# A row-maximum kernel: the first load as two transfers, partitions 0 to 15 and then 16 to 127

## The chip, the core and the metric

The kernel runs on one core of a Trainium2 chip. The metric is the time of one execution on the device, in microseconds (us). Runs of the kernel before agree to less than 0.1 us.

## The reference

The input is a float32 array of 32 x 512 x 1024, and the output is its maximum along the last axis:

```python
def reference(x):
    return np.max(x, axis=-1).astype(np.float32)
```

Flattened, there are 16,384 rows of 1024 numbers, 67.1 MB, and one number comes out of each row.

## The kernel before, in words

The rows are spread over 128 partitions, 128 rows for each partition. `BLOCKS` (lines 13 to 16) cuts these 128 into a first block of 112 and a second of 16. Within a block each partition owns consecutive rows of the input, so a load of n rows per partition reads n x 4096 consecutive bytes for each partition. In the first block the loads have 14, 13, 12, 11, 9, 8, 8, 7, 6, 5, 5, 4, 4, 3 and 3 rows per partition, in the second 2, 2, 2 and then nine times 1; the last row of each partition is loaded in two halves.

All loads but the very last half go into `ring` (line 39), a buffer with place for 45 rows per partition. Each load takes the next n places; where they would run over the end, it begins at place 0 again. So the loads of 14, 13 and 12 rows (39 places) fit side by side, and the load of 11 begins at the start again, where the 14 rows lay.

The loop at lines 53 to 60 goes over the loads. Line 57 issues a load from the queue of the sync engine (SP); line 58 takes its maximum on the vector engine (DVE) with one instruction into `res`. SP issues loads in the order of the program. A load whose places were used before waits for the reduction that read them; this is why the load of 11 rows waits for the first reduction. The framework gives the transfers eight completion semaphores in turn, so a transfer also waits for the one eight before it. DVE reduces the loads in the same order, each as soon as its load has landed.

At the end, lines 64 to 70 load and reduce the last row in two halves, and the ACT queue stores `res` in two pieces, 56 KB (line 73) and 8 KB (line 75).

The lines in question are:

```python
            xc = ring[:, at:at + n, :]
            nc.sync.dma_start(out=xc, in_=xb[:, b:b + n, :])
            reduce = nc.vector.reduce_max(out=res[:, first + b:first + b + n], in_=xc, axis=X)
```

Of the kernel before, what the change touches and what calls it, by code (L numbers as in the profile page):

```python
# [1 line left out]

# [4 lines left out]


F32 = mybir.dt.float32

BLOCKS = [
    [14, 13, 12, 11, 9, 8, 8, 7, 6, 5, 5, 4, 4, 3, 3],
    [2, 2, 2, 1, 1, 1, 1, 1, 1, 1, 1, 1],
]
RING = 45
SYNC = mybir.DependencyInfo(mybir.DependencyClass.Sync, mybir.DependencyReason.DATA)


@with_exitstack
def kernel(
    ctx: ExitStack,
    tc: tile.TileContext,
    x: bass.AP,
    out: bass.AP,
):
    nc = tc.nc
    P = 128
    X = mybir.AxisListType.X  # L30

    xf = x.flatten_outer_dims()
    N, D = xf.shape
    H = D // 2
    I = N // P
    of = out.flatten_outer_dims()

    once = ctx.enter_context(tc.tile_pool(name="once", bufs=1))
    ring = once.tile([P, RING, D], F32)
    res = once.tile([P, I], F32)  # L40

    PAD = 16
    tail = once.tile([P, PAD + H], F32)

    at = first = 0
    views = []
    for loads in BLOCKS:
        S = sum(loads) + (loads is BLOCKS[-1])
        xb = xf[first * P:(first + S) * P, :].rearrange("(p i) d -> p i d", p=P)
        dst = bass.AP(tensor=of.tensor, offset=of.offset + first * P, ap=[[S, P], [1, S]])  # L50
        views.append((dst, res[:, first:first + S]))
        b = 0
        for n in loads:
            if at + n > RING:
                at = 0
            xc = ring[:, at:at + n, :]
            nc.sync.dma_start(out=xc, in_=xb[:, b:b + n, :])  # L57
            reduce = nc.vector.reduce_max(out=res[:, first + b:first + b + n], in_=xc, axis=X)  # L58
            at += n
            b += n  # L60
        first += S
    assert first == I

    if at + 1 > RING:
        at = 0
    half = ring[:, at, :H]
    nc.sync.dma_start(out=half, in_=xb[:, b, :H])
    nc.sync.dma_start(out=tail[:, PAD:], in_=xb[:, b, H:])
    nc.vector.reduce_max(out=tail[:, PAD - 1:PAD], in_=half, axis=X)  # L69
    nc.vector.reduce_max(out=res[:, I - 1:], in_=tail[:, PAD - 1:], axis=X)  # L70


    store = nc.scalar.dma_start(out=views[0][0], in_=views[0][1])
    tc.add_manual_dep(store.ins, reduce.ins.name, SYNC, reason="behind the loads")
    nc.scalar.dma_start(out=views[1][0], in_=views[1][1])


# [1 line left out]
_INS = ['x']  # L79
_OUTS = [((32, 512), 'float32')]  # L80


# [23 lines left out]
```

## Time and profile before

| What | Value |
|---|---|
| Median of 3 runs | 164.99 us (164.98 to 165.05) |
| The profiled execution | 165.17 us |
| Span of its profile, first to last instruction | 163.4 us |
| DVE busy | 139.0 us, 85% of the span |
| Bytes read | 67.11 MB, 411 GB/s over the span |
| First load | 7168 KB, 19.6 us from issue to landing |
| First reduction starts | at 20.31 us, takes 15.09 us |

Times in the profile count from the start of the span. "Busy" is the time in which an engine executed. The sync engine is shown as SPq where it issues transfers; those instructions are not counted as busy. The arrow in a line such as `res<-ring` reads from right to left, output from input. A transfer is cut into packets, and here a packet of the first load is the whole of one partition's part, 57,344 bytes. In the windows a packet is counted with all its bytes where it starts, so short windows go above what the hardware can move and then show zero; only a stretch of several microseconds has a true rate.

### The profile page before, as it was taken

Reading aid. Unit: us, or ns where it says so; the run is one execution under the profiler, and the core shown is the slowest. Engines: PE = TensorE matmul, PEld = TensorE weight load, DVE = VectorE, ACT = ScalarE, POOL = GpSimd, SP = SyncE. Lnnn points to the kernel's source line nnn. Section 1 sums busy time; section 2 is a strip of 40 time slices with the busy share of each in tenths; the row PEclk is TensorE's granted clock in tenths of the full one; section 3 lists DMA queues with packets and bytes.
Section 4 is the critical chain, followed back from the end, with each engine's and each line's share of the span. In section 5 each row is a group of like instructions: output and inputs, shape, how many; then the busy total and the mean of one; then the engine's idle time right before and its main releaser. Section 6 shows DMA issues by size and latency. Waiting matters only on the chain.

```text
span 163.4 us, 117 instructions
## 1 busy us (share of the span) xinstructions
DVE 139.0 (85%) x29; POOL 0.2 (0%) x4
## 2 busy tenths in 40 slices
DVE  0000099989998999999999999999999999999994
POOL 0000000000000000000000000000000000000000
DMA  6999999999989989999989999999999999999990
GB/s 225 449 449 449 433 417 417 417 401 529 433 385 430 452 386 432 433 433 441 457 385 481 401 442 422 409 438 421 446 409 425 437 410 422 427 407 409 409 355 16
DMA packets 4464, 67.18 MB, mean 411 GB/s; under 512 B 752, under 2 KB 752, under 8 KB 2160
## 3 DMA queue, kind: packets, MB, share of 16 engines
q1 hardware_dynamic: 4176, 67.11, 96.6%
q10 hardware_dynamic: 288, 0.07, 0.2%
HBM read 67.11 MB, written 0.07 MB: 411 GB/s over the span
## 4 chain that ended last, share of the span: by engine, by line
DVE 49%; DMA 48%; SPq 1%; issue 0%
DMA ring<-in_x_dram 48%; DVE res L58 48%; SPq L57 1%; DVE res L70 0%; DVE tail L69 0%
## 5 line engine op out<-in xcount | busy, mean ns | idle before, releaser
L58 DVE TENSOR_REDUCE res<-ring 128x1 f32<-128x1024 f32 (+12 forms) x27 | 137.7, 5165 | 22.1 <-DMA ring<-in_x_dram 22.1
L70 DVE TENSOR_REDUCE res<-tail 128x1 f32<-128x513 f32 x1 | 0.7, 686 | 0.0
L69 DVE TENSOR_REDUCE tail<-ring 128x1 f32<-128x512 f32 x1 | 0.7, 682 | 0.0
L90 POOL MEMSET const-bfloat16-1.0<- 128x1 bf16 x1 | 0.1, 102 | 0.0
L90 POOL MEMSET const-uint8-127<- 128x1 uint8 x1 | 0.1, 102 | 0.0
L90 POOL MEMSET const-float32-0.0<- 128x1 f32 x1 | 0.1, 99 | 0.2 <-issue 0.2
L90 POOL MEMSET const-float32-1.0<- 128x1 f32 x1 | 0.1, 99 | 0.0
## 6 DMA issues: line engine op xcount, KB each, us to landing
ring<-in_x_dram SPq DMA_DIRECT2D x2, 4096.0 KB, 25.6
ring<-in_x_dram SPq DMA_DIRECT2D x1, 7168.0 KB, 19.6
ring<-in_x_dram SPq DMA_DIRECT2D x1, 6656.0 KB, 34.9
ring<-in_x_dram SPq DMA_DIRECT2D x1, 6144.0 KB, 48.9
ring<-in_x_dram SPq DMA_DIRECT2D x1, 5632.0 KB, 28.5
ring<-in_x_dram SPq DMA_DIRECT2D x2, 2560.0 KB, 38.4
ring<-in_x_dram SPq DMA_DIRECT2D x1, 4608.0 KB, 24.7
ring<-in_x_dram SPq DMA_DIRECT2D x9, 512.0 KB, 13.8
```

Of the source, the lines that this page charges most:

```text
L57: nc.sync.dma_start(out=xc, in_=xb[:, b:b + n, :])
L58: reduce = nc.vector.reduce_max(out=res[:, first + b:first + b + n], in_=xc, axis=X)
L69: nc.vector.reduce_max(out=tail[:, PAD - 1:PAD], in_=half, axis=X)
L70: nc.vector.reduce_max(out=res[:, I - 1:], in_=tail[:, PAD - 1:], axis=X)
L90: nc = _bacc.Bacc("TRN2", target_bir_lowering=False, num_devices=1)
```

## The change

For the first load alone (the load of 14 rows), line 57 becomes two transfers from the same queue: first partitions 0 to 15, then partitions 16 to 127. With 16 partitions each of the sixteen DMA engines may get one descriptor. The reduction of the first load now waits for both. All other loads stay as they are, and so do all reductions. The program has one transfer more on the sync engine's queue, and the completion semaphores that the later transfers use move on by one.

```diff
             xc = ring[:, at:at + n, :]
-            nc.sync.dma_start(out=xc, in_=xb[:, b:b + n, :])
+
+            for p, q in ((0, 16), (16, P)) if first + b == 0 else ((0, P),):
+                nc.sync.dma_start(out=xc[p:q], in_=xb[p:q, b:b + n, :])
             reduce = nc.vector.reduce_max(out=res[:, first + b:first + b + n], in_=xc, axis=X)
```

## The prediction

> **What bounds the kernel now.** I read the chain of waits first, then the waits, then the timeline, and last the windows over the first microseconds.
>
> ```profile
> DVE 49%; DMA 48%; SPq 1%; issue 0%
> ...
> DVE res L58 <- DMA ring<-in_x_dram: 22.1, 5, 20.3
> ...
> 20.31 15.09 DVE L58 TENSOR_REDUCE res<-ring 128x14 f32<-128x14336 f32 x1 [20.31 <-DMA ring<-in_x_dram]
> 36.05 14.02 DVE L58 TENSOR_REDUCE res<-ring 128x13 f32<-128x13312 f32 x1 [0.65 <-DMA ring<-in_x_dram]
> 50.58 12.95 DVE L58 TENSOR_REDUCE res<-ring 128x12 f32<-128x12288 f32 x1 [0.51 <-DMA ring<-in_x_dram]
> 63.91 30.14 DVE L58 TENSOR_REDUCE res<-ring 128x11 f32<-128x11264 f32 x3 [0.38 <-DMA ring<-in_x_dram]
> 94.27 65.48 DVE L58 TENSOR_REDUCE res<-ring 128x8 f32<-128x8192 f32 x21 [0.21 <-DMA ring<-in_x_dram]
> ...
> ring<-in_x_dram SPq DMA_DIRECT2D x1, 7168.0 KB, 19.6
> ```
>
> The first line is the chain's split: half VectorE (DVE), half transfers. The second says that of DVE's 22.1 us of waiting on loads, 20.3 is one wait, for the first load. The timeline shows what follows: from 20.31 on DVE reduces almost without a break (gaps of 0.65, 0.51, 0.38 and 0.21, together 1.75 us) until 160. So the end is the landing of the first load plus about 141 us of DVE work and four small gaps. One microsecond on the first landing is one microsecond on the end, unless the 1.75 us of gaps absorb some of it. The last line is that load's 19.6 us from issue (at 0.73) to landing.
>
> How are these 19.6 us made up? The windows have columns window, length, DVE busy, POOL busy, clock, DMA share, GB/s; a packet is put at its start.
>
> ```profile
> 1.25:1.50 0.25, 0.00 (x0) 0.00 (x0) 1.00 0.00 0
> 1.50:1.75 0.25, 0.00 (x0) 0.00 (x0) 1.00 2.98 918
> 1.75:2.00 0.25, 0.00 (x0) 0.00 (x0) 1.00 4.59 1376
> 2.00:2.25 0.25, 0.00 (x0) 0.00 (x0) 1.00 1.39 459
> 2.25:2.50 0.25, 0.00 (x0) 0.00 (x0) 1.00 1.19 459
> 2.50:2.75 0.25, 0.00 (x0) 0.00 (x0) 1.00 1.07 459
> 2.75:3.00 0.25, 0.00 (x0) 0.00 (x0) 1.00 0.00 0
> ...
> 4.00:8.00 4.00, 0.00 (x0) 0.00 (x0) 1.00 1.06 459
> ```
>
> A row of the first load is one partition's 14 x 1024 x 4 = 57,344 bytes. One such packet in a quarter microsecond reads 229 GB/s, so the five filled windows hold 4, 6, 2, 2 and 2 packets: all sixteen DMA engines start their first row between 1.5 and 2.75 us. After that the stream is full: 459 GB/s at a share of 1.06 is 433 GB/s at share 1, or 27.1 per engine, so **a row takes 57,344 / 27.1 = 2.12 us**. 128 rows on 16 engines are 8 rows each, 16.9 us. Issue 0.73, first packets about 1 us later, 16.9 us of rows, and some 1.3 us of stagger and slow first rows give the landing near 20; DVE starts at 20.31.
>
> [...]
>
> **The change part by part.**
>
> *First piece, 16 rows[...].* [...] I take 8.46.
>
> *Second piece, 112 rows, seven to each engine.* [...] How the rows are dealt out isn't in the trace. I take contiguous sevens: engine e writes partitions 16+7e to 22+7e. [...] I take the middle of 10.6 and 14.8, 12.7, and take off 0.7, about half of the 1.3 us of stagger and slow first rows[...]: **+12.0**.
>
> *One more issue on SP.* An issue takes 0.37 to 0.43 us with 0.05 between (chain: 0.73, 1.15, 1.63). The second piece goes out at about 1.15, the loads of 13 and 12 at about 1.6 and 2.1. The sixteen engines have rows until 17 us at least; that covers it, cost 0. Without this cover 0.42. The load of 11 still waits for the first reduce; it now waits on two transfers as well, landed by then.
>
> *One more wait on DVE.* The first reduce waits for two transfers. If that takes an instruction of its own it is like SP's wait instructions at L57, 17 ns: 0.02. Everything else on DVE is queued behind it and stays in order and size.
>
> *What the delay does later.* Fast engines hold three loads and can't run dry: the load of 11 goes out after the first reduce, near 47 us, before any engine is through its 39 rows per partition (20.4 MB, 47 us at 433 GB/s, after the 6 us lost on its first row). The late engines set the second landing too, so I expect the gap of 0.65 to stay and no delay to be given back; at most 1.75 us would be. DVE's 139 us stay. Late next is every reduce, by the same amount.
>
> Sum: 163.4 + 12.0 = 175.4 of span. The profiled execution took 165.17, so 177.2; the median of the runs is 164.99, 0.18 below it, so 177.0.
>
> **Rivals.** *[...]better dealt:* if the second piece's rows meet no more than they must, the cost is 8.5 - 0.7 = +7.8, 172.8. [...] *The change doesn't do what it says:* the first piece is given to four engines, four rows each, and those then have 11 rows: 23.3 us, +6.4, 171.4. [...] *Other side, faster:* [...] sixteen single rows are handed out faster than 128. Then the stagger between 1.5 and 2.75 us shrinks; it holds at most 1.3 us, and I price it at 0.6: 164.4. It decides if the first piece's rows take about 2.1 us; from 2.7 us a row on (2.12 + 0.6) the gain is gone. For: the first issue takes 371 ns against 327 of others[...]. *No change:* [...] the starts stay staggered, 165.0. *Dealt sixteen at a time:* 8 x 8.46 = 67.7 us, +50.8, 215.8.
>
> **How the numbers follow.** A measurement of this kernel can tell about 0.2% (0.3 us) from no change. Contiguous sevens 0.50 (174.5 to 183.5); better dealt 0.20 (171.5 to 174.5); four engines 0.10 (169.5 to 171.5); sixteen at a time 0.06; faster 0.08; no change 0.06. Slower is 0.50 + 0.20 + 0.10 + 0.06 = 0.86. The likeliest gives 177.0. The range 169.5 to 183.5 holds the first three, 0.80.
>
> **What would show it.** In the changed profile: the first piece lands 9 to 11 us after its issue (wrong if 3 to 4); few bytes start in the windows from 3 to 9 us; the second piece lands near 32; the first reduce starts near 32.3; the four later gaps are as now; the last reduce ends 12 us later. A first reduce within half a microsecond of 20.31 makes the whole argument wrong. A first piece of 9 to 11 us with a first reduce at 28 means better dealing; near 70, sixteen at a time. A late first reduce with a smaller shift of the end would mean that the gaps gave some back.

## The result, and the profile after

The changed kernel takes 183.71 us (median of 6 runs, 183.31 to 184.32) against 165.02 before (6 runs, 164.87 to 165.15): a ratio of 1.114, 95% interval 1.112 to 1.116, **18.7 us slower**. I forecast 177.0 and a range up to 183.5, so the direction was right and the size was not: 12.0 us were forecast, 18.7 came, and the time lies 0.2 us above the range.

The views of the changed kernel that answer to those of before are, in this order, the split of the chain, DVE's wait for loads, the timeline of the first reductions and the issues of the second and the first piece:

```profile
DVE 60%; DMA 37%; another core or an unknown queue 1%; SPq 0%; issue 0%; DVEq 0%
...
DVE res L60 <- DMA ring<-in_x_dram: 40.6, 5, 39.0
...
38.98 15.09 DVE L60 TENSOR_REDUCE res<-ring 128x14 f32<-128x14336 f32 x1 [38.98 <-DMA ring<-in_x_dram]
54.63 14.02 DVE L60 TENSOR_REDUCE res<-ring 128x13 f32<-128x13312 f32 x1 [0.57 <-DMA ring<-in_x_dram]
69.16 12.95 DVE L60 TENSOR_REDUCE res<-ring 128x12 f32<-128x12288 f32 x1 [0.51 <-DMA ring<-in_x_dram]
82.49 30.14 DVE L60 TENSOR_REDUCE res<-ring 128x11 f32<-128x11264 f32 x3 [0.38 <-DMA ring<-in_x_dram]
112.84 65.46 DVE L60 TENSOR_REDUCE res<-ring 128x8 f32<-128x8192 f32 x21 [0.21 <-DMA ring<-in_x_dram]
...
ring<-in_x_dram SPq DMA_DIRECT2D x1, 6272.0 KB, 37.7
...
ring<-in_x_dram SPq DMA_DIRECT2D x1, 896.0 KB, 10.6
```

The "unknown queue" in the first line is the gaps of about half a microsecond ahead of the second and the third reduction, for which the timeline names the loads. All of the loss lies ahead of the first reduction. It starts at 38.98 instead of 20.31, 18.67 later; every duration and every later gap is as before, but for the gap of 0.65, which is 0.57. So 0.1 us is given back, and the span is 18.5 longer. The first piece lands 10.6 us after its issue, where I expected 9 to 11. The second lands 37.7 us after its issue, at 38.9, where I expected 32. The excess is in the second piece.

The windows say more. "Row" is meant here as in the forecast, one partition's part of the load. A step is sixteen rows that start together, as many as there are DMA engines. A window that holds all sixteen starts of one step has 16 x 57,344 bytes in it, so GB/s times length is about 918. Then the DMA share times the length is the **mean duration of a row** in that step. For the kernel before, the first two steps:

```profile
1.40:2.90 1.50, 0.00 (x0) 0.00 (x0) 1.00 1.87 612
4.40:5.30 0.90, 0.00 (x0) 0.00 (x0) 1.00 2.35 1019
```

These are 1.87 x 1.50 = 2.81 us and 2.35 x 0.90 = 2.12 us; the first row is slower than those that follow. The eight steps of the changed kernel, the 16-row piece first, then the seven of the 112-row piece:

```profile
1.40:2.90 1.50, 0.00 (x0) 0.00 (x0) 1.00 4.96 612
...
8.50:10.30 1.80, 0.00 (x0) 0.00 (x0) 1.00 2.59 510
13.50:14.50 1.00, 0.00 (x0) 0.00 (x0) 1.00 4.12 918
17.60:18.60 1.00, 0.00 (x0) 0.00 (x0) 1.00 2.98 918
20.60:22.80 2.20, 0.00 (x0) 0.00 (x0) 1.00 1.51 417
23.90:26.00 2.10, 0.00 (x0) 0.00 (x0) 1.00 1.87 437
27.50:30.00 2.50, 0.00 (x0) 0.00 (x0) 1.00 1.62 367
31.50:34.00 2.50, 0.00 (x0) 0.00 (x0) 1.00 1.57 367
```

The row means are 7.4, then 4.7, 4.1, 3.0, 3.3, 3.9, 4.1 and 3.9 us. A row of the second piece takes 3.9 us, 1.8 times the normal 2.12, **on the mean of all engines**. The rows within a step differ too. By the packets of the trace, in the step at 13.50 all sixteen took 4.09 to 4.25 us. In the one at 17.60 two took 4.19 and fourteen 2.60 to 2.99, in the one at 20.60 two took 3.79 and 3.87 and the others 3.23 to 3.38. These are the two short steps: only they have two late rows and a faster rest.

So the theory to test: (a) the second piece is dealt out in contiguous sevens; (b) the cost comes from which partitions are written in the same step; (c) some sets of sixteen partitions slow all their rows, others only two of them. The rivals: another dealing, with worse sets; a cost in reading memory; a cost of having more transfers; and for (c), that the slow rows are always only those that are in each other's way, as I had counted.

In the expectations a pair is two rows of a step that I took to be in each other's way, and the sharers are the rows of such pairs. Which partitions make pairs was my assumption. No trace or run here shows it, and what follows goes by the sets of partitions and the row times measured for them.

### The profile page after: what moved, and what is told of

Its sections match the earlier page's. It is cut to its first block, busy times and chain, and to the rows that moved or that the text cites. A ratio compares the mean times of both kernels' runs of the same rounds, so it can differ in the third digit from the quotient of the medians.

```text
span 181.9 us, 119 instructions
## 1 busy us (share of the span) xinstructions
DVE 138.9 (76%) x29; POOL 0.2 (0%) x4
## 4 chain that ended last, share of the span: by engine, by line
DVE 60%; DMA 37%; another core or an unknown queue 1%; SPq 0%; issue 0%; DVEq 0%
DVE res L60 59%; DMA ring<-in_x_dram 37%; SPq L59 0%; DVE res L72 0%; DVE tail L71 0%; DVEq L60 0%
## 6 DMA issues: line engine op xcount, KB each, us to landing
ring<-in_x_dram SPq DMA_DIRECT2D x1, 6272.0 KB, 37.7
```

## Experiments

Each time is the median of 4 runs, of 13 for the split by rows.

**Dealing: the sevens written out.** The 112 rows as seven transfers of 16 partitions at a step of 7:

```diff
-            for p, q in ((0, 16), (16, P)) if first + b == 0 else ((0, P),):
-                nc.sync.dma_start(out=xc[p:q], in_=xb[p:q, b:b + n, :])
+            parts = [slice(0, P)]
+            if first + b == 0:
+                parts = [slice(0, 16)] + [slice(16 + j, 122 + j, 7) for j in range(7)]
+            for s in parts:
+                nc.sync.dma_start(out=xc[s], in_=xb[s, b:b + n, :])
```

> Tests how the 112 rows are dealt out. The second piece becomes seven transfers, each of 16 partitions at a step of 7 (16+j, 23+j, ... 121+j), so that each engine's rows are contiguous sevens by construction. If the changed kernel deals contiguous sevens too, this is the same traffic and takes the same time, 183.7 us within 0.5. If it deals them out otherwise, there is no reason for the same time[...].

Measured: 184.10 us (183.87 to 184.68), 0.4 above the changed kernel, with six more transfers. The windows of its third to fifth step (the 16-row piece is the first):

```profile
13.70:15.10 1.40, 0.00 (x0) 0.00 (x0) 1.00 2.97 655
17.80:19.30 1.50, 0.00 (x0) 0.00 (x0) 1.00 1.98 612
20.85:23.50 2.65, 0.00 (x0) 0.00 (x0) 1.00 1.35 346
```

They give 4.2, 3.0 and 3.6 us, against 4.1, 3.0 and 3.3 in the changed kernel: a long step and then two shorter ones in both. The single transfer of 112 partitions behaves as contiguous sevens: (a) holds, as far as times can tell.

**Partitions: eight sixteens, contiguous and spread.** Both kernels load the first 14 rows as eight transfers of 16 partitions, from the same source rows. One writes partitions 16r to 16r+15, the other every eighth:

```diff
-            for p, q in ((0, 16), (16, P)) if first + b == 0 else ((0, P),):
-                nc.sync.dma_start(out=xc[p:q], in_=xb[p:q, b:b + n, :])
+            parts = [(slice(0, P), slice(0, P))]
+            if first + b == 0:
+                parts = [(slice(r, P, 8), slice(16 * r, 16 * r + 16)) for r in range(8)]
+            for s, t in parts:
+                nc.sync.dma_start(out=xc[s], in_=xb[t, b:b + n, :])
```

(the contiguous kernel has `slice(16 * r, 16 * r + 16)` on both sides). By (b) I expected 215 us contiguous and 181 spread.

> The first load as eight transfers of 16 contiguous partitions. [...] 8.46 us, eight steps 67.7 instead of 16.9, so +50.8 less about 1 us of start: 215. Theory '[...]the cost is in reading memory or in the number of transfers': eight rows per engine as before, 165 to 170.

> As the kernel with eight transfers of 16 partitions, with the same sixteen source rows in each transfer, but written to every eighth partition (r, r+8, ... r+120), so the output comes in another order. [...] 4.23 us a step, eight steps 33.9, +16.9 less about 1: 181. Theory 'the reading side': nothing has changed on the side of memory, so the same time as with contiguous partitions.

Measured: 212.35 us contiguous (ratio 1.287, 1.285 to 1.289) and 184.39 spread (1.118, 1.116 to 1.119). One step from the middle of each, contiguous first:

```profile
16.20:18.50 2.30, 0.00 (x0) 0.00 (x0) 1.00 3.47 399
```

```profile
10.60:12.10 1.50, 0.00 (x0) 0.00 (x0) 1.00 2.98 612
```

That is 8.0 us a row with contiguous partitions, and 4.5 with every eighth. The same reads cost 28 us more or less according to the partitions they are written to, so the cost is on the side that writes SBUF. (b) holds. The sizes of a row were a little off, in opposite directions: 8.46 and 4.23 were expected (four and two times 2.12; the factors were my assumption), and 215 and 181 us in all. As a rate, 16 x 57,344 bytes in 8.0 us are 115 GB/s, in 4.5 us 204, against 433 in the kernel before.

**Reading side: another source pitch.** The change, with the source rows packed:

```diff
-                nc.sync.dma_start(out=xc[p:q], in_=xb[p:q, b:b + n, :])
+                src = xb[p:q, b:b + n, :]
+                if first + b == 0:
+                    src = xf[:P * n, :].rearrange("(p i) d -> p i d", p=P)[p:q]
+                nc.sync.dma_start(out=xc[p:q], in_=src)
```

> The changed kernel with another source for the two pieces: the first 1792 rows of x, packed (partition p reads 57,344 bytes at a pitch of 57,344 in place of 458,752), so the values of the first load are not the right ones. Destinations as in the change. [...] nothing changes, 183.7 within 0.7. Theory 'the reading side' (several engines reading rows that lie at a bad distance): the second piece gets faster, anything down to 165.

Measured: 183.93 us (183.54 to 184.50). The distance between the rows in memory plays no part that shows.

**One more transfer, with all 128 partitions in both.** The first load split by rows of the input, so that both transfers have all 128 partitions:

```diff
-            for p, q in ((0, 16), (16, P)) if first + b == 0 else ((0, P),):
-                nc.sync.dma_start(out=xc[p:q], in_=xb[p:q, b:b + n, :])
+            parts = [(0, n)]
+            if first + b == 0:
+                parts = [(0, 1), (1, n)]
+            for p, q in parts:
+                nc.sync.dma_start(out=xc[:, p:q, :], in_=xb[:, b + p:b + q, :])
```

> The first load as two transfers again, but split by rows: all 128 partitions, first 1 row, then 13. One transfer more on the queue and two waits for the first reduction, as in the change[...]. If the second transfer or its wait itself costs, it shows here: +0.3 or more. [...] within 0.2 us of the kernel before, 165.0.

Measured: 164.94 us, ratio 0.9996 (0.9988 to 1.0004); the first reduction starts at 20.20:

```profile
20.20 15.09 DVE L63 TENSOR_REDUCE res<-ring 128x14 f32<-128x14336 f32 x1 [20.20 <-DMA ring<-in_x_dram]
```

The second transfer and the second wait cost nothing that can be measured, and a small piece in front gains nothing either. This also sets aside the thought behind "one descriptor for each engine" in this form: with all 128 partitions, a short first piece brings the first reduction forward by 0.1 us in the profile, and the end not measurably.

**Which rows are slowed: probes with three sets of partitions.** In front of the unchanged first load I put four transfers of 16 partitions times 7 rows of x, at a step of 7, always from the same source rows. Between the three probes only the starting partition differs (here 11, for which I expected no pair; from 3 I expected one, from 2 two):

```diff
+        if first == 0:
+            for j in range(4):
+                to = ring[11:117:7, 14 + 7 * j:21 + 7 * j, :]
+                nc.sync.dma_start(out=to, in_=xb[0:16, 7 * j:7 * j + 7, :])
```

> The kernel before with four extra transfers ahead of the first load, each of 16 partitions times 7 rows (28,672 bytes per partition), to partitions 11, 18, ... 116 (step 7) of a part of the ring that is overwritten later. [...] 1.06 us a row, four rows 4.2 us: about 169.2, mean packet 1.06 us.

> The same from partition 3 (3, 10, ... 108)[...]; source rows as before. Theory 'only the sharers': their rows take 2.12 us, the others' 1.06, mean packet 1.19 us; the late two set the end, at most 8.5 us for four rows, 173.4. Theory 'all are slowed': the others take longer as well, mean packet 1.45 to 1.6 us[...].

> The same from partition 2 (2, 9, ... 107)[...]. Theory 'only the sharers': mean packet 1.33 us. Theory 'all are slowed': mean packet 2.0 to 2.1 us[...]. The end is about 173 in both.

Measured: 170.65, 174.53 and 173.66 us (before: 164.94). The windows over the second of the four transfers (a row is 28,672 bytes, so sixteen starts are 459), from 11, 3 and 2:

```profile
3.55:4.25 0.70, 0.00 (x0) 0.00 (x0) 1.00 1.62 655
```

```profile
3.45:4.30 0.85, 0.00 (x0) 0.00 (x0) 1.00 1.44 540
```

```profile
3.60:4.70 1.10, 0.00 (x0) 0.00 (x0) 1.00 1.89 417
```

The means are 1.13, 1.22 and 2.08 us. From 3 the mean is that of "only the sharers" (1.19 was expected). From 2 it is that of "all are slowed"; "only the sharers" would give 1.33. Neither of my two theories had both. Note that the end does not tell the cases apart: from 3 it is 174.53 us, even longer than the 173.66 from 2. Only the mean row does. (In the third of the four transfers rows took 1.55 us on the mean even from 11, and there the first reduction starts at 26.32, 6.0 us later than in the kernel before, where four rows of 1.06 are 4.2. I don't know why, so something other than the set of partitions can slow a row too. I read the second transfer for that reason, and the next probes have longer rows.)

**Longer rows: four sets of partitions.** Four probes now, with two extra transfers and rows of 57,344 bytes as in the change; only the partitions differ. Two sets go at a step of 7 (from 11 and from 4), two at a step of 6 (from 4 and from 16). For the sets at a step of 6 there are two theories: "number", that both slow all their rows, and "halves", that the one from 4 slows four rows and leaves twelve at 2.12. That one:

```diff
+        if first == 0:
+            for j in range(2):
+                to = ring[4:95:6, 14 + 14 * j:28 + 14 * j, :]
+                nc.sync.dma_start(out=to, in_=xb[0:16, 14 * j:14 * j + 14, :])
```

> Two extra transfers ahead of the first load, each of 16 partitions times 14 rows (57,344 bytes per partition, as in the change), to partitions 11, 18, ... 116[...]. The second of the two is the one to read, since the first carries the start. Mean packet 2.12 us in it; two rows 4.2 us, about 169.5 in all.

> The same to partitions 4, 11, ... 109[...]. If one pair slows only itself, as the one-pair probe with shorter rows suggested in its second transfer, the second transfer has a mean packet of (2 x 4.23 + 14 x 2.12) / 16 = 2.38 us; if it slows all, up to 4.2.

> The same to partitions 4, 10, ... 94[...]. Theory 'number': two pairs are what slows all engines, mean packet 4.2 us in the second transfer. Theory 'halves': [...] the twelve others keep 2.12 here and the mean is (4 x 4.23 + 12 x 2.12) / 16 = 2.65 us.

> The same to partitions 16, 22, ... 106[...]. Both theories: all engines slowed, mean packet 4.1 to 4.2 us in the second transfer.

Measured: 170.43, 175.11, 174.23 and 174.40 us (before: 165.01). The windows over the second transfer, in this order; for the second probe, the fourteen early starts and the two late ones apart:

```profile
4.80:5.90 1.10, 0.00 (x0) 0.00 (x0) 1.00 1.94 834
```

```profile
4.90:6.10 1.20, 0.00 (x0) 0.00 (x0) 1.00 1.60 669
6.10:6.40 0.30, 0.00 (x0) 0.00 (x0) 1.00 2.54 382
```

```profile
5.30:7.80 2.50, 0.00 (x0) 0.00 (x0) 1.00 1.79 367
```

```profile
5.40:7.40 2.00, 0.00 (x0) 0.00 (x0) 1.00 2.24 459
```

From 11 at a step of 7: 1.94 x 1.10 = 2.13 us. From 4 at a step of 7: fourteen rows (669 x 1.20 is 14 rows of bytes) with a mean of 1.60 x 1.20 x 16/14 = 2.19, and two with 2.54 x 0.30 x 16/2 = 6.1; fourteen rows keep their pace. From 4 at a step of 6: 4.48. From 16 at a step of 6: 4.48. So "halves" is out. In both sets at a step of 6 the mean row takes about twice the 2.13 (4.1 us in the changed kernel's step at 13.50, where all sixteen do), and the spread sixteens, at 4.5 us, are no worse. The part of (c) on sets that slow all their rows holds.

The part on two late rows holds in these probes only, and two places in the traces speak against it as a rule. The first is what follows in the probe from 4 at a step of 7. Its two late rows took 6.1 us, where I expected 4.2. By then the other engines had begun the first load, and its first fourteen rows have a mean of 1.44 x 2.00 x 16/14 = 3.29 us:

```profile
6.60:8.60 2.00, 0.00 (x0) 0.00 (x0) 1.00 1.44 401
```

One of them, which starts at 7.11 us, took 5.9, while the rest took 2.9 to 3.2. Three rows of about 6 us, three times 2.0, would fit three rows in each other's way; that they are isn't shown, since the trace does not give a packet's partition. The ten rows that start next belong to a load whose rows take 2.12 us in the kernel before, and they need 2.54 x 0.65 x 16/10 = 2.64:

```profile
10.10:10.75 0.65, 0.00 (x0) 0.00 (x0) 1.00 2.54 882
```

If so, a few rows in each other's way slowed the engines of the other rows. The second place is the changed kernel. In its step at 17.60 two rows take 4.2 us, twice 2.1, but the others take 2.6 to 3.0. Part of that is the step before, whose last row ends at 18.57. But the row that starts just then took 2.32 x 0.07 x 16 = 2.60:

```profile
18.53:18.60 0.07, 0.00 (x0) 0.00 (x0) 1.00 2.32 819
```

The rows of the next step, from 20.75 us on, can account for the last 0.4 us of this row only. Why two late rows cost the others something here and nothing in the second transfer of the probe isn't shown.

## Why the prediction was right or wrong

**The bound: right.** The end followed the first landing nearly one to one: 18.67 us at the first reduction, 18.5 in the span. The four gaps stayed but for 0.1 us, as did DVE's work.

**First piece: right.** The 8.46 us a row was an estimate of mine, with a factor of four over 2.12 that the trace before didn't show; measured were 7.4 in this kernel, where the sixteen rows start within 1.5 us, as many as there are engines, and 8.0 in a later step of the contiguous sixteens. Why the first step is the shorter of the two isn't shown. Its landing, 10.6 us after issue, fell in the range given. The second piece did not pass it: no row starts between 2.7 and 8.5 us.

**Dealing: right.** The sevens were assumed; writing them out gave the same time and the same pattern of steps.

**Second piece: the step that failed** is "I take the middle of 10.6 and 14.8". Both ends were estimates of mine from assumed pairs, and that count lets the rows of a pair slow only each other. Beside 8.46 for the first piece they leave 10.6 + 16.9 - 8.5 = 19.0 and 14.8 + 16.9 - 8.5 = 23.2 us for the second. The seven steps measured 4.7 + 4.1 + 3.0 + 3.3 + 3.9 + 4.1 + 3.9 = 27.0 us on the mean of all engines; at the pace of the kernel before seven rows take 14.8. In five of the steps all sixteen rows were slow, 3.6 to 5.0 us, and in the two short ones the rows beside the two late ones were slowed too, if less, to 2.6 to 3.4. The addition for early engines running on into the second load, 2.1 on the middle, could not make up for this: the first engines did run on, at 35.5 us, but the last rows of the late ones took 4.1 us, no longer than rows in the steps before.

The sum with the measured terms: rows after 7.4 + 27.0 = 34.4, before 2.8 + 14.8 = 17.6, a difference of 16.8 on the mean row. The first reduction came 18.7 later. The 1.9 between them is lateness behind the mean. By the packets of the two traces the last row of the load ends 1.8 us after the mean one here and 0.35 before, which is 1.4; from the end of the last row to the start of the reduction it is 0.86 us here and 0.36 before, which is 0.5.

Twice the normal time for every row of the second piece, 7 x 4.23 = 29.6 us, would have been the better guess, since in effect most rows were slowed nearly that much.

**One more issue and one more wait: right.** The split by rows prices both together at nothing that can be measured. The wait shows in the chain of the changed kernel as an instruction of 0.02 us on DVE's queue, the price that I had put on it, with 0.05 us of issue behind it:

```profile
38.91 0.02 DVEq L60
```

**Rivals.** Four are excluded. Better dealing: by the sevens, and by a cost above its 7.8. Four engines for the first piece: sixteen rows of 7.4 us start within 1.5 us. Sixteen at a time: its steps would take 8 us each. Rows as fast with 16 partitions as with 128, which "faster" and "no change" need: by the two kernels of eight sixteens.

Left open: what makes a set of partitions slow, why some sets slow all sixteen rows and others two, and when two late rows cost the others something. The probes show that two sets at a step of 6 do the same, and that at a step of 7 the start decides. They don't show the cause. Open too is what slowed the third transfer of the probe with short rows from 11.

## What to carry to other kernels

Split a large load along the free dimension, not over partitions: one row of all 128 partitions ahead of 13 cost nothing, 16 partitions ahead of 112 cost 18.7 us. Where partitions must be split, measure the rows of each set of sixteen that is written together. A row that takes 2.12 us in a load of all 128 partitions took 2.13 at a step of 7 from 11, about 4.5 at a step of 6 or with every eighth, and 8.0 with sixteen contiguous ones. In a slow set price every row of the step at that time, not only a few. With only two late rows, the other rows took from 2.2 to 3.4 us here. And where a load is the first that everything waits for, its landing goes into the end microsecond for microsecond.

## What was not expected of the hardware

Sets of partitions at a step of 6 took about 4.5 us a row on the mean of all sixteen, against 2.13 from 11 at a step of 7, though the forecast had let only some rows of a step be late. The set from 4 at a step of 7 left fourteen rows at 2.19 in the probe, but in the changed kernel a row beside two late ones took 2.60. And the contiguous sixteens took less than twice the row time of the spread ones, 8.0 us against 4.5, where I had expected 8.46 and 4.23.
